# Seven products in three of four column groups of the down product, with sums carried in PSUM by ScalarE

## The chip, the cores and the metric

The kernel runs on one core of one Trainium2 chip. The metric is the device time of one execution in microseconds; the time before is the median of three runs, 1151.33 us (1150.51 to 1153.75). A profile was taken of one further execution.

## The reference

One layer on 256 tokens plus 16 meta tokens, model width 2048, everything in float32. Attention (differential and stick-breaking heads) comes first; the change leaves it alone apart from where its tables lie. What follows it is what matters here:

```python
m = _rmsnorm(h, g_mlp[l])
hid = jnp.square(jax.nn.relu(jnp.einsum('bld,df->blf', m, w_up[l])))   # 2048 -> 8192
h = h + jnp.einsum('blf,fd->bld', hid, w_down[l])                      # 8192 -> 2048
```

## The kernel before

**Precision.** Every float32 operand is split into a high part, rounded by ScalarE (a cast, L169), and a low part, what is left of it, by VectorE (a subtraction, L171). A product is then three matmuls: high by high, low by high and high by low. In the names, `raw` is a loaded block of weights (128 x 1024 values), `whi` and `wlo` its two parts, `m` the normalised input, `hid` the hidden values.

**Stages.** First the projections and attention, then the output product (L1038 with `out`), then the MLP. The MLP is cut into 8 rounds of 1024 hidden columns. In a round, four strips of `up` products (L1032) make the hidden values, each strip from four blocks of weights; `down` products (L1038) take the round's hidden values times the weights of four column groups u = 0 to 3 of the output, four blocks each. I call a block of up weights **c**, and a block of down weights in a plain group **d**: 24 matmuls 256 wide for c, 12 matmuls 512 wide for d.

**Seven products.** For the groups in `FAST`, a 2 x 2 block product is done with seven products in place of eight (`fast_a`, `fast_b`). A loaded block gives two sets of parts: **a** (the three blocks as they are, 9 matmuls 256 wide) and **b** (four sums of blocks, made by VectorE in L267 to L271 in place in `raw`, 12 matmuls 256 wide). The hidden values need four more sums for it (`up_evac`, L856 to L860), which all strips make. The seven results of a group stand in four PSUM banks. After a round, `fast_evac` moves them out: ScalarE copies them to the tile `z` in the first round (L896), VectorE adds them to `z` in all others (L899). After the last round `combine` turns the seven sums into four and adds them to the residual `H` (L918, L922). A plain group is added to `H` by VectorE every round (`plain_evac`, L876).

**Order.** All engines run in an order that is written when the program is built. TensorE follows the list `order`; in a round the next round's up blocks lie between the down blocks of this one. `Pace` counts expected times of the engines and puts the jobs of ScalarE and VectorE (casts, subtractions, evacuations) into their queues accordingly; each engine then works strictly through its queue. A block's parts go into one of `MLP_PARTS` sets of buffers, in turn: the first three sets come from the pool `weights`, the others from the pool `mlp`. The cast of block g waits until TensorE has done block g - MLP_PARTS. Loads are issued by SyncE, five `raw` buffers in turn.

**Tables.** The tile `cst` (identity, rotation tables, masks) lies in the pool `const`, which stays to the end; the pool `temps` is given up after attention.

Of the kernel before, what the change touches and what calls it, by code (L numbers as in the profile page):

```python
# [21 lines left out]
ROUNDS = 8  # L22
PAIRS = 4
# [2 lines left out]
KINDS = ((0, 3, 1, 2, 4, 5), (1, 0, 2, 4, 3, 5), (1, 0, 2, 4, 3, 5), (1, 0, 4, 3, 2, 5))  # L26
PARTS = 3
LEAD = 2
MLP_PARTS = 5
MLP_LEAD = 4  # L30
FAST = {(r, u) for r in range(ROUNDS) for u in (0, 2)}
PSUM_BANKS = {"acc": 4, "att": 4}
SLOTS = {"k": 4, "q": 4, "v": 2, "e": 3, "pr": 2, "ah": 2, "m": 2, "n": 2}
K0 = META + P
# [1 line left out]
SW = K0 + TOK  # L36
SEG = (slice(TOK, SW), slice(0, TOK))

C_ID, C_COS, C_SIN, C_MD, C_MS, C_BLK, C_SEL, C_END = 0, 128, 400, 672, 800, 1216, 1344, 1346
G_MIX, G_MLP, G_Q, G_K, G_D, G_S, G_L, G_END = 0, 16, 32, 33, 34, 35, 36, 292  # L40


# [77 lines left out]
def hymba_layer(ctx: ExitStack, tc: tile.TileContext, xT_d, xh_d, win_d, wout_d, wup_d, wdn_d, cst_d, par_d, out_d):  # L120
    nc = tc.nc
    cp = ctx.enter_context(tc.tile_pool(name="const", bufs=1))
# [15 lines left out]
    def bank(tag, name):  # L138
        return ps.tile([P, 512], F32, tag=tag, bufs=PSUM_BANKS[tag], name=name)
# [12 lines left out]


    par = cp.tile([P, G_END], F32, name="par")
    cst = cp.tile([P, C_END], F32, name="cst")
    xT = big.tile([P, KT, TOK], F32, tag="x", name="xT")
    um = big.tile([P, KT, 2, TOK], F32R, tag="act", name="u")
    mixed = big.tile([P, KT, 2, SEQ], F32R, tag="mix", name="mixed")
# [36 lines left out]
    for i in range(PAIRS):
        order += up(0, i, range(4))
    for r in range(ROUNDS):
        for u in (0, 2):
            ab, d = down(r, u, range(PAIRS)), down(r, u + 1, range(PAIRS))
            if r < ROUNDS - 1:  # L200
                c = up(r + 1, u, range(4)) + up(r + 1, u + 1, range(4))
                for p in range(PAIRS):
                    order += [c[2 * p], ab[2 * p], c[2 * p + 1], ab[2 * p + 1], d[p]]
            else:
                order += [*ab[:4], d[0], *ab[4:6], d[1], *ab[6:], *d[2:]]
    index = {key: g for g, key in enumerate(order)}
    loads = [g for g, key in enumerate(order) if key[0] != "b"]
    load_of = {g: n for n, g in enumerate(loads)}
# [90 lines left out]
    for c in range(4):  # L299
        n = 2 if c == 0 else 4  # L300
# [8 lines left out]

    def constants():  # L310
        yield from later(RAW)
        pc.at["cst"] = load(cst, cst_d, C_END)
        load(par[:, G_L:], par_d[:, G_L:], G_END - G_L)
        for g in range(RAW + 1, LEAD + RAW):
            pc.job("fetch", later(g))


    ident = cst[:, C_ID : C_ID + P]
    cos = cst[:, C_COS : C_COS + TOK]
    sin = cst[:, C_SIN : C_SIN + TOK]  # L320
    maskd = cst[:, C_MD : C_MD + P]
    masks = cst[:, C_MS : C_MS + SW]
    blk64 = tp.tile([P, P], F32R, bufs=1, name="blk64")
    sel = cst[:, C_SEL : C_SEL + 2]
    ones = cp.tile([P, P], F32R, name="ones")
    gqk = tp.tile([P, 2], F32, bufs=1, name="gqk")
    gout = cp.tile([P, 2], F32, name="gout")
    nlam = cp.tile([P, 1], F32, name="nlam")
# [553 lines left out]

    LAST_FAST = {u: max(r for r, v in FAST if v == u) for u in {u for _, u in FAST}}

    def fast_evac(r, u, o):

        new = u not in Z
        if new:
            Z[u] = mtile(f"z{u}", [P, 7 * 256], f"z_{u}")
        z = Z[u]  # L890
        yield pc.pe, "a" if new else "v"
        for i in range(4):
            n = 512 if i < 3 else 256
            dst = z[:, 512 * i : 512 * i + n]
            if new:
                nc.scalar.copy(dst, o[i][:, :n])  # L896
                t = pc.A(n)
            else:
                nc.vector.tensor_tensor(dst, o[i][:, :n], dst, op=ALU.add)  # L899
                t = pc.V(n)  # L900
            pc.give("att", t)
            yield pc.pe, "a" if new else "v"
# [25 lines left out]
    def banks(tag, n, name):  # L928
        while sum(t <= pc.pe for t in pc.banks[tag]) < n:
            pc.pe += 100  # L930
            pc.pump()
        pc.banks[tag] = sorted(pc.banks[tag])[n:]
        return [bank(tag, f"{name}_{j}") for j in range(n)]
# [36 lines left out]
        yield from gen  # L970
        pc.give("e", max(pc.pe, pc.dve, pc.act) + pc.WAIT)

    idle = cp.tile([P, 512], mybir.dt.bfloat16, name="idle")
    nc.vector.memset(idle, 0.0)
    warm = bank("att", "warm")
    for _ in range(WARM):
# [94 lines left out]
    for g in range(first_mlp, len(order)):  # L1071
        what, r, u, p = order[g]
        begin(g, MLP_LEAD)
        hi, lo = parts[g]
        pc.stall(("w", g, 3))
        if what == "up":
            if p == 0:
                open_strips["up", r, u] = banks("acc", 1, f"up_{r}_{u}")[0]
            o = open_strips["up", r, u]
            for j in range(2):  # L1080
                for kk in range(4):
                    k = 2 * p + kk % 2 + 8 * (kk // 2)
                    pc.stall(("m", k))
                    w = [x[:, kk, P * j : P * j + P] for x in (hi, lo)]
                    t = triple2(o[:, SEQ * j : SEQ * j + SEQ], w, m[:, k], p == 0 and kk == 0 and j == 0, p == 3 and kk == 3)
                    pc.pump()
            if p == 3:
                pc.job("evac", after(t, up_evac(r, u, o)))
        else:
            fast = (r, u) in FAST  # L1090
            pc.stall(("hid", r, p))
            x = lambda slot: [hid[r][:, p, slot, a] for a in range(2)]
            if p == 0 and what == "a":
                open_strips["down", r, u] = banks(*(("att", 4) if fast else ("acc", 2)), f"down_{r}_{u}")
# [81 lines left out]
```

## Time and profile before

| | |
|---|---|
| median of three runs | 1151.33 us |
| the profiled execution, its own time | 1152.82 us |
| its span, first to last instruction | 1150.9 us |
| TensorE busy | 1133.8 us, 8383 matmuls |
| VectorE busy | 928.1 us, 1420 instructions |
| ScalarE busy | 710.1 us, 1103 instructions |
| mean granted TensorE clock | 0.995 |

The MLP's matmuls run from 433.5 us to 1145.1 us of the span. A busy TensorE is not a TensorE at its peak, since the profile's matmuls overlap; the start-to-start distance of matmuls is the better measure. "Idle before" is the time in which an engine waited, and the name after the arrow is what it waited for.

### The profile page before, as it was taken

The page shows a single profiled execution, that of the slowest core. Times are in us where ns is not written, and L with a number is a line of the kernel's source. Part 1 is how long each engine was busy: PE and PEld are TensorE (multiplying, and loading weights), DVE is VectorE, ACT ScalarE, POOL GpSimd, SP SyncE. Part 2 cuts the span into 40 slices and gives each one's busy share as a digit, 9 for nine tenths or more (in the row PEclk, how much of TensorE's full clock was granted, in tenths as well). Part 3 has the DMA queues.
Part 4 walks back from the last instruction along what each step waited for, and adds up shares of the span by engine and source line. Part 5 has one row for each costly group of instructions (what it writes and reads, how often), then busy time and mean ns, then how long its engine had stood idle before and what let it go on. Part 6 is the DMA issues. An engine that isn't in the chain of part 4 may idle for free. (4 is left out here: it accounts for less than half of the span.)

```text
span 1150.9 us, 21193 instructions
## 1 busy us (share of the span) xinstructions
PE 1133.8 (99%) x8383; PEld 1076.6 (94%) x8383; DVE 928.1 (81%) x1420; ACT 710.1 (62%) x1103; POOL 1.1 (0%) x8
## 2 busy tenths in 40 slices
PE   9999999999999999999999999999999999999987
PEld 8999999999998889999999999999999999999876
DVE  6987987987976556677878888888888888888788
ACT  7769888778776445556655555555555555555542
POOL 0000000000000000000000000000000000000000
PEclk9999999999999999999999999999999999999989
DMA  8564544554545555556566666566666656666543
GB/s 326 184 220 142 153 139 151 156 155 153 164 139 175 183 185 191 172 185 201 189 196 201 188 191 200 192 188 204 192 189 200 195 188 199 196 191 196 171 136 122
DMA packets 57987, 209.97 MB, mean 182 GB/s; under 512 B 6560, under 2 KB 6688, under 8 KB 57760
## 3 DMA queue, kind: packets, MB, share of 16 engines
q1 hardware_dynamic: 57888, 208.61, 57.1%
q8 instruction: 66, 1.08, 0.4%
q14 instruction: 33, 0.27, 0.1%
HBM read 206.49 MB, written 2.10 MB: 181 GB/s over the span
## 5 line engine op out<-in xcount | busy, mean ns | idle before, releaser
L169 ACT CAST whi<-raw 128x1024 fp32r<-128x1024 f32 (+2 forms) x454 | 455.8, 1008 | 374.8 <-PE up L1032 198.7
L171 DVE TENSOR_TENSOR wlo<-raw,whi 128x1024 fp32r<-128x1024 f32 (+2 forms) x454 | 525.2, 1170 | 171.7 <-ACT whi L169 154.3
L1032 PE MATMUL up<-m,whi 128*128 128x256 f32 x2048 | 366.2, 281 | 1.3 <-DVE m L813 0.9
L1038 PE MATMUL down<-whi,hid 128*128 128x256 f32 (+1 forms) x1408 | 324.2, 324 | 7.1 <-DVE z L899 7.1
L1032 PEld LDWEIGHTS up<-m,whi 128*128 128x128 f32 x2048 | 319.3, 190 | 6.8 <-DVE m L813 1.6
L1032 PE MATMUL up<-m,wlo 128*128 128x256 f32 x1024 | 287.3, 281 | 0.0
L1038 PEld LDWEIGHTS down<-whi,hid 128*128 128x128 f32 x1408 | 232.3, 191 | 25.8 <-issue 3.6
L1038 PE MATMUL down<-wlo,hid 128*128 128x256 f32 (+1 forms) x704 | 228.1, 324 | 0.9 <-DVE wlo L171 0.9
L947 PE MATMUL acc<-u,whi 128*128 128x272 f32 (+1 forms) x768 | 224.6, 292 | 0.4 <-ACT whi L169 0.4
L949 PE MATMUL acc<-u,wlo 128*128 128x272 f32 (+1 forms) x768 | 221.0, 288 | 0.2 <-DVE wlo L171 0.2
L948 PE MATMUL acc<-u,whi 128*128 128x272 f32 (+1 forms) x768 | 220.6, 287 | 0.0
L1032 PEld LDWEIGHTS up<-m,wlo 128*128 128x128 f32 x1024 | 194.9, 190 | 0.0
L947 PEld LDWEIGHTS acc<-u,whi 128*128 128x128 f32 x768 | 145.9, 190 | 2.3 <-ACT whi L169 1.3
L949 PEld LDWEIGHTS acc<-u,wlo 128*128 128x128 f32 x768 | 145.6, 190 | 0.7 <-DVE wlo L171 0.7
L948 PEld LDWEIGHTS acc<-u,whi 128*128 128x128 f32 x768 | 146.2, 190 | 0.0
L1038 PEld LDWEIGHTS down<-wlo,hid 128*128 128x128 f32 x704 | 134.2, 191 | 11.9 <-DVE wlo L171 1.1
L1038 PE MATMUL out<-whi,mixed 128*128 128x512 f32 x256 | 79.8, 393 | 0.0
L1038 PEld LDWEIGHTS out<-whi,mixed 128*128 128x128 f32 x256 | 47.2, 188 | 9.3
L1038 PE MATMUL out<-wlo,mixed 128*128 128x512 f32 x128 | 50.0, 390 | 0.0
L267 DVE TENSOR_TENSOR raw<-raw 128x512 f32<-128x512 f32 x64 | 44.3, 692 | 2.2
L868 DVE TENSOR_TENSOR hid<-hx,hid 128x1024 fp32r<-128x1024 f32 x32 | 38.9, 1216 | 0.0
L899 DVE TENSOR_TENSOR z<-down,z 128x512 f32<-128x512 f32 (+1 forms) x56 | 34.0, 615 | 0.0
(241 smaller groups left out, 844.4 us busy)
## 6 DMA issues: line engine op xcount, KB each, us to landing
raw<-in_wup SPq DMA_DIRECT2D x128, 512.0 KB, 3.6
raw<-in_wdn SPq DMA_DIRECT2D x128, 512.0 KB, 4.4
raw<-in_win SPq DMA_DIRECT2D x95, 512.0 KB, 3.7
raw<-in_wout SPq DMA_DIRECT2D x32, 512.0 KB, 3.5
H<-in_xh SPq DMA_DIRECT2D x1, 2048.0 KB, 8.3
out<-H SPq DMA_DIRECT2D x8, 256.0 KB, 2.1
xT<-in_x SPq DMA_DIRECT2D x3, 544.0 KB, 9.6
cst<-in_cst SPq DMA_DIRECT2D x1, 673.0 KB, 11.2
```

The lines of the kernel that those rows point to most:

```text
L169: nc.scalar.copy(hi, src)
L171: nc.vector.tensor_tensor(lo, src, as32(hi), op=ALU.subtract)
L267: nc.vector.tensor_tensor(raw[:, 3::-3], first, raw[:, 3:1:-1], op=ALU.add)
L868: nc.vector.tensor_tensor(lo, x, as32(hi), op=ALU.subtract)
L899: nc.vector.tensor_tensor(dst, o[i][:, :n], dst, op=ALU.add)
L947: nc.tensor.matmul(o, lhsT=h, rhs=xh, start=first, stop=False)
L948: nc.tensor.matmul(o, lhsT=h, rhs=xl, start=False, stop=False)
L949: nc.tensor.matmul(o, lhsT=l, rhs=xh, start=False, stop=last)
L1032: nc.tensor.matmul(out, lhsT=w[a], rhs=x[:, b], start=first and i == 0, stop=last and i == 2, skip_group_check=True)
L1038: nc.tensor.matmul(out, lhsT=x[a], rhs=w[b], start=first and i == 0, stop=last and i == 2, skip_group_check=check)
```

## The change

`FAST` holds groups 0, 1 and 2 in rounds 0 to 6 and group 0 alone in round 7: 22 pairs of round and group, 16 before. The order of blocks is a string of letters per group; in round 0 two strips are woven into each other, and the last round begins with two plain blocks and ends with two. The parts of blocks go into four sets of buffers, five before, and are made three blocks ahead, four before. A third tile `z` takes the place. The sums of a group over the rounds no longer grow in `z` by VectorE's additions: ScalarE copies the finished banks to `z` of this group and copies the `z` of the next group into the same banks, and the matmuls go on adding there, with no start flag after round 0. The tables, `ones` and `idle` move to `temps`; only the identity stays.

```diff
-MLP_PARTS = 5
-MLP_LEAD = 4
-FAST = {(r, u) for r in range(ROUNDS) for u in (0, 2)}
+MLP_PARTS = 4
+MLP_LEAD = 3
+FAST = {(r, u) for r in range(ROUNDS - 1) for u in range(3)} | {(ROUNDS - 1, 0)}
...
-    cst = cp.tile([P, C_END], F32, name="cst")
+    cst = tp.tile([P, C_ID], F32, bufs=1, name="cst")
+    ident = cp.tile([P, P], F32, name="ident")
...
-                c = up(r + 1, u, range(4)) + up(r + 1, u + 1, range(4))
-                for p in range(PAIRS):
-                    order += [c[2 * p], ab[2 * p], c[2 * p + 1], ab[2 * p + 1], d[p]]
-            else:
-                order += [*ab[:4], d[0], *ab[4:6], d[1], *ab[6:], *d[2:]]
+    order += up(0, 0, range(3)) + up(0, 1, range(3)) + up(0, 0, (3,)) + up(0, 1, (3,)) + up(0, 2, range(4)) + up(0, 3, range(4))
+    for r in range(ROUNDS - 1):
...
+        for u, mix in ((0, "cdcabcabcabcab"), (1, "cdcabcabcabcab"), (2, "cdcabcabcdabccab")):
...
+    order += [next({"d": d, "a": ab, "b": ab}[x]) for x in "dd" + "adbd" * 4 + "dd"]
...
+        after = fast_units[fast_units.index((r, u)) + 1 :][:1]
+        for i in AT:
...
+            yield pc.pe, "a"
+            nc.scalar.copy(Z[u][:, at], o[i][:, :n])
...
+            for r2, u2 in after:
+                new[i] = bank("att", f"down_{r2}_{u2}_{i}")
+                if u2 in Z:
+                    nc.scalar.copy(new[i][:, :n], Z[u2][:, at])
...
-                               p == 0 and (at, half) in ((0, 0), (1, 0), (3, 0), (2, 1)), p == PAIRS - 1, True)
+                               r == 0 and p == 0 and (at, half) in ((0, 0), (1, 0), (3, 0), (2, 1)), p == PAIRS - 1, True)
```

Three places show what moves. The first is VectorE's queue in the middle of a round, where the sums of an up strip's hidden values (`hx`) come by. Blocks are numbered from 128, where the MLP begins. Before, in round 2, 235 is an a, 237 its b, 236 and 238 are c and d:

```order
L171 TENSOR_TENSOR wlo_235_8360<-raw_235_8251,whi_235_8359 128x768
L267 TENSOR_TENSOR raw_235_8251<-raw_235_8251 128x2x256
L269 TENSOR_TENSOR raw_235_8251<-raw_235_8251 128x256
L271 TENSOR_TENSOR raw_235_8251<-raw_235_8251 128x256
L171 TENSOR_TENSOR wlo_236_8394<-raw_236_8313,whi_236_8393 128x1024
L171 TENSOR_TENSOR wlo_237_8411<-raw_235_8251,whi_237_8410 128x1024
L856 TENSOR_TENSOR hx_3_0_8405<-hx_3_0_8405 128x2x128
L858 TENSOR_TENSOR hx_3_0_8405<-hx_3_0_8405 128x128
L860 TENSOR_TENSOR hx_3_0_8405<-hx_3_0_8405 128x128
L171 TENSOR_TENSOR wlo_238_8434<-raw_238_8320,whi_238_8433 128x1024
L868 TENSOR_TENSOR hid_3_8455<-hx_3_0_8405,hid_3_8455 128x8x128
```

Here the b's subtraction (`wlo_237`) is ahead of the hidden sums, and another subtraction lies between these and `hid`. VectorE's queue in the changed kernel, at the same place in round 3, where 299 is an a, 300 its b and 301 a c:

```order
L172 TENSOR_TENSOR wlo_299_9858<-raw_299_9711,whi_299_9857 128x768
L268 TENSOR_TENSOR raw_299_9711<-raw_299_9711 128x2x256
L270 TENSOR_TENSOR raw_299_9711<-raw_299_9711 128x256
L272 TENSOR_TENSOR raw_299_9711<-raw_299_9711 128x256
L857 TENSOR_TENSOR hx_4_1_9868<-hx_4_1_9868 128x2x128
L859 TENSOR_TENSOR hx_4_1_9868<-hx_4_1_9868 128x128
L861 TENSOR_TENSOR hx_4_1_9868<-hx_4_1_9868 128x128
L172 TENSOR_TENSOR wlo_301_9893<-raw_301_9778,whi_301_9892 128x1024
L172 TENSOR_TENSOR wlo_300_9874<-raw_299_9711,whi_300_9873 128x1024
L869 TENSOR_TENSOR hid_4_9659<-hx_4_1_9868,hid_4_9659 128x8x128
```

The three sums of hidden values stand ahead of both subtractions, of which the later, `wlo_300`, is what TensorE needs first, and its own subtraction `hid` comes right behind it.

The second place is the evacuation of group 0. Before, in round 2, VectorE does it, with other work in between:

```order
L899 TENSOR_TENSOR z_0_6735<-down_2_0_0_8233,z_0_6735 128x512
L171 TENSOR_TENSOR wlo_247_8645<-raw_245_8494,whi_247_8644 128x1024
L856 TENSOR_TENSOR hx_3_1_8639<-hx_3_1_8639 128x2x128
L858 TENSOR_TENSOR hx_3_1_8639<-hx_3_1_8639 128x128
L860 TENSOR_TENSOR hx_3_1_8639<-hx_3_1_8639 128x128
L899 TENSOR_TENSOR z_0_6735<-down_2_0_1_8234,z_0_6735 128x512
L171 TENSOR_TENSOR wlo_248_8666<-raw_248_8554,whi_248_8665 128x1024
L899 TENSOR_TENSOR z_0_6735<-down_2_0_2_8235,z_0_6735 128x512
L868 TENSOR_TENSOR hid_3_8455<-hx_3_1_8639,hid_3_8455 128x8x128
L171 TENSOR_TENSOR wlo_249_8702<-raw_249_8584,whi_249_8701 128x1024
L899 TENSOR_TENSOR z_0_6735<-down_2_0_3_8236,z_0_6735 128x256
```

The four additions are spread over VectorE's row. In the changed kernel, in round 3, it stands in ScalarE's queue between two casts (293 is an a, 294 its b):

```order
L170 CAST whi_293_9701<-raw_293_9586 128x768
L900 COPY z_0_6602<-down_3_0_0_9387 128x512
L905 COPY down_3_1_0_9714<-z_1_6926 128x512
L900 COPY z_0_6602<-down_3_0_1_9403 128x512
L905 COPY down_3_1_1_9730<-z_1_6926 128x512
L900 COPY z_0_6602<-down_3_0_3_9423 128x256
L905 COPY down_3_1_3_9747<-z_1_6926 128x256
L900 COPY z_0_6602<-down_3_0_2_9452 128x512
L905 COPY down_3_1_2_9753<-z_1_6926 128x512
L170 CAST whi_294_9741<-raw_293_9586 128x1024
```

Four additions of VectorE have become eight copies of ScalarE, four out of PSUM and four into it, in one row; VectorE has none of it left.

The third place is the end of VectorE's queue, behind the MLP's last weights (`z_2` is group 2, `down_7_3` the last plain group). Before:

```order
L876 SCALAR_TENSOR_TENSOR H_1128<-down_7_1_1_13052,R2_116,H_1128 128x512
L899 TENSOR_TENSOR z_2_7214<-down_7_2_0_13211,z_2_7214 128x512
L899 TENSOR_TENSOR z_2_7214<-down_7_2_1_13212,z_2_7214 128x512
L899 TENSOR_TENSOR z_2_7214<-down_7_2_2_13213,z_2_7214 128x512
L899 TENSOR_TENSOR z_2_7214<-down_7_2_3_13214,z_2_7214 128x256
L918 TENSOR_TENSOR z_2_7214<-z_2_7214 128x256 x7
L922 SCALAR_TENSOR_TENSOR H_1128<-z_2_7214,R2_116,H_1128 128x256 x4
L876 SCALAR_TENSOR_TENSOR H_1128<-down_7_3_0_13278,R2_116,H_1128 128x512
L876 SCALAR_TENSOR_TENSOR H_1128<-down_7_3_1_13279,R2_116,H_1128 128x512
```

The last fast group's evacuation and sums come ahead of the last plain additions. VectorE's queue in the changed kernel, at its end:

```order
L172 TENSOR_TENSOR wlo_469_13809<-raw_469_13745,whi_469_13808 128x1024
L172 TENSOR_TENSOR wlo_470_13825<-raw_470_13730,whi_470_13824 128x1024
L172 TENSOR_TENSOR wlo_471_13844<-raw_471_13764,whi_471_13843 128x1024
L924 TENSOR_TENSOR z_0_6602<-z_0_6602 128x256 x7
L928 SCALAR_TENSOR_TENSOR H_1130<-z_0_6602,R2_117,H_1130 128x256 x4
L877 SCALAR_TENSOR_TENSOR H_1130<-down_7_3_0_13826,R2_117,H_1130 128x512
L877 SCALAR_TENSOR_TENSOR H_1130<-down_7_3_1_13827,R2_117,H_1130 128x512
```

The last group's evacuation and sums, which stood behind the last subtraction of weights, are those of group 0 now, whose matmuls end three plain blocks before the last; behind them stand only the two additions of a plain group.

More of the change, by code (lines that the diff above doesn't have):

```diff
@@ L37 @@
 SEG = (slice(TOK, SW), slice(0, TOK))
-C_ID, C_COS, C_SIN, C_MD, C_MS, C_BLK, C_SEL, C_END = 0, 128, 400, 672, 800, 1216, 1344, 1346
+C_COS, C_SIN, C_MD, C_MS, C_BLK, C_SEL, C_ID, C_END = 0, 272, 544, 672, 1088, 1216, 1218, 1346
 G_MIX, G_MLP, G_Q, G_K, G_D, G_S, G_L, G_END = 0, 16, 32, 33, 34, 35, 36, 292
@@ L193, in down @@
         return [(x, r, u, p) for p in ps for x in ("ab" if (r, u) in FAST else "a")]
[L195 to L200, printed above, removed]
-                c = up(r + 1, u, range(4)) + up(r + 1, u + 1, range(4))
-                for p in range(PAIRS):
-                    order += [c[2 * p], ab[2 * p], c[2 * p + 1], ab[2 * p + 1], d[p]]
-            else:
-                order += [*ab[:4], d[0], *ab[4:6], d[1], *ab[6:], *d[2:]]
+    order += up(0, 0, range(3)) + up(0, 1, range(3)) + up(0, 0, (3,)) + up(0, 1, (3,)) + up(0, 2, range(4)) + up(0, 3, range(4))
+    for r in range(ROUNDS - 1):
+        c = iter([key for i in range(PAIRS) for key in up(r + 1, i, range(4))])
+        d = iter(down(r, 3, range(PAIRS)))
+        for u, mix in ((0, "cdcabcabcabcab"), (1, "cdcabcabcabcab"), (2, "cdcabcabcdabccab")):
+            ab = iter(down(r, u, range(PAIRS)))
+            order += [next({"c": c, "d": d, "a": ab, "b": ab}[x]) for x in mix]
+        assert not [*c, *d]
+    ab = iter(down(ROUNDS - 1, 0, range(PAIRS)))
+    d = iter([key for u in (1, 2, 3) for key in down(ROUNDS - 1, u, range(PAIRS))])
+    order += [next({"d": d, "a": ab, "b": ab}[x]) for x in "dd" + "adbd" * 4 + "dd"]
     index = {key: g for g, key in enumerate(order)}
@@ L311, in constants @@
         yield from later(RAW)
-        pc.at["cst"] = load(cst, cst_d, C_END)
+        pc.at["cst"] = load(cst, cst_d[:, :C_ID], C_ID)
+        load(ident, cst_d[:, C_ID : C_ID + P], P)
         load(par[:, G_L:], par_d[:, G_L:], G_END - G_L)
@@ L315, in constants @@
             pc.job("fetch", later(g))
-    ident = cst[:, C_ID : C_ID + P]
     cos = cst[:, C_COS : C_COS + TOK]
@@ L324, in hymba_layer @@
     sel = cst[:, C_SEL : C_SEL + 2]
-    ones = cp.tile([P, P], F32R, name="ones")
+    ones = tp.tile([P, P], F32R, bufs=1, name="ones")
     gqk = tp.tile([P, 2], F32, bufs=1, name="gqk")
@@ L883, in hymba_layer @@
     LAST_FAST = {u: max(r for r, v in FAST if v == u) for u in {u for _, u in FAST}}
+    fast_units = sorted(FAST)
+    AT = (0, 1, 3, 2)
     def fast_evac(r, u, o):
-        new = u not in Z
-        if new:
+        if u not in Z:
             Z[u] = mtile(f"z{u}", [P, 7 * 256], f"z_{u}")
[L890 to L902, printed above, removed]
+        after = fast_units[fast_units.index((r, u)) + 1 :][:1]
+        for r2, u2 in after:
+            open_strips["down", r2, u2] = new = {}
+        for i in AT:
+            at = slice(512 * i, min(512 * i + 512, 7 * 256))
+            n = at.stop - at.start
+            yield pc.pe, "a"
+            nc.scalar.copy(Z[u][:, at], o[i][:, :n])
+            t = pc.A(n)
+            for r2, u2 in after:
+                new[i] = bank("att", f"down_{r2}_{u2}_{i}")
+                if u2 in Z:
+                    nc.scalar.copy(new[i][:, :n], Z[u2][:, at])
+                    t = pc.A(n)
+        for key in after:
+            pc.at["seed", *key] = t
         if r == LAST_FAST[u]:
@@ L971, in delayed @@
         pc.give("e", max(pc.pe, pc.dve, pc.act) + pc.WAIT)
-    idle = cp.tile([P, 512], mybir.dt.bfloat16, name="idle")
+    idle = tp.tile([P, 512], mybir.dt.bfloat16, bufs=1, name="idle")
     nc.vector.memset(idle, 0.0)
@@ L1093, in hymba_layer @@
             if p == 0 and what == "a":
-                open_strips["down", r, u] = banks(*(("att", 4) if fast else ("acc", 2)), f"down_{r}_{u}")
+                if fast and (r, u) == fast_units[0]:
+                    open_strips["down", r, u] = dict(zip(AT, banks("att", 4, f"down_{r}_{u}")))
+                elif fast:
+                    pc.stall(("seed", r, u))
+                else:
+                    open_strips["down", r, u] = banks("acc", 2, f"down_{r}_{u}")
             o = open_strips["down", r, u]
```

## The prediction

> **What bounds the kernel now.** I first read the busy times of the page:
>
> ```profile
> PE 1133.8 (99%) x8383; PEld 1076.6 (94%) x8383; DVE 928.1 (81%) x1420; ACT 710.1 (62%) x1103; POOL 1.1 (0%) x8
> ```
>
> TensorE works nearly all the time. Second I cut the time from the MLP's first matmul on into four stretches: the first round's up products, rounds 0 to 6, round 7, and what is left behind the last matmul. The columns are length, then busy time of PE, PEld, DVE, ACT and POOL, the granted clock, the DMA share and GB/s.
>
> ```profile
> 433.50:483.90 50.40, 49.08 (x394) 48.07 (x393) 32.18 (x42) 27.62 (x35) 0.00 (x0) 0.97 0.53 176
> 483.90:1088.60 604.70, 604.70 (x4527) 576.23 (x4526) 498.47 (x628) 337.52 (x371) 0.00 (x0) 1.00 0.62 194
> 1088.60:1145.10 56.50, 48.39 (x278) 42.37 (x276) 52.94 (x83) 22.46 (x25) 0.00 (x0) 0.94 0.37 122
> 1145.10:1150.90 5.80, 0.00 (x0) 0.00 (x0) 2.69 (x6) 0.00 (x0) 0.00 (x0) 0.94 0.49 181
> ```
>
> In rounds 0 to 6 TensorE never waits (604.70 of 604.70): time changes there only if matmuls go away, if they follow each other faster or slower, or if a wait comes that isn't there now. VectorE is busy for 82%, ScalarE for 56%. In round 7 VectorE is busy for 52.94 of 56.50 and TensorE waits: there VectorE is the bound.
>
> Third the timeline of TensorE, for the length of one block of each kind (start to start):
>
> ```profile
> 700.83 0.40 PE L1032 MATMUL up<-m,whi 128*128 128x256 f32 x2
> 701.06 0.28 PE L1032 MATMUL up<-m,wlo 128*128 128x256 f32 x1
> ...
> 703.70 0.40 PE L1038 MATMUL down<-whi,hid 128*128 128x256 f32 x2
> ...
> 704.78 0.39 PE L1032 MATMUL up<-m,whi 128*128 128x256 f32 x2
> ...
> 707.50 0.40 PE L1038 MATMUL down<-whi,hid 128*128 128x256 f32 x2
> ...
> 708.92 0.63 PE L1038 MATMUL down<-whi,hid 128*128 128x512 f32 x2
> ...
> 711.68 0.40 PE L1032 MATMUL up<-m,whi 128*128 128x256 f32 x2
> ```
>
> c 2.87, a 1.08, the second c 2.72, b 1.42, d 2.76 (2.77 over the round). The two c are the same 24 matmuls. The first has its parts in a set of buffers of the pool `weights`, the second in one of the pool `mlp`.
>
> **The change, part by part.** The sum is made against the profiled execution, 1152.82 us; its span is 1150.9, and the median of the runs is 1.49 lower.
>
> *Start.* Round 0's fourth up block waits for the last rows of `m`:
>
> ```profile
> PEld up L1032 <- DVE m L813: 1.6, 3, 1.1
> PE up L1032 <- DVE m L813: 0.9, 1, 0.9
> PEld up L1032 <- ACT m L811: 0.7, 2, 0.5
> PE up L1032 <- ACT m L811: 0.3, 1, 0.3
> ```
>
> These are 3.5 us, and the granted clock of this stretch is .97, so .03 x 50.4 = 1.5 are lost to slow matmuls besides. The new order puts three blocks of the second strip ahead of that block, 3 x 2.87 = 8.6 us of work that needs none of these rows and covers the wait. Between -3.5 and -5.0 I take -4.0, since some of the low clock may have another cause.
>
> *Pace in rounds 0 to 6.* Seven more groups are fast. Each trades four d, 4 x 2.77 = 11.08, for four a and b, 4 x (1.08 + 1.42) = 10.00: 7 x 1.08 = -7.6. Against it, four sets in place of five, three of `weights` and one of `mlp`: by the order, 62 of the 128 c lie in sets of `mlp` before and 18 after. 44 c at 2.87 in place of 2.72 are +6.6. Together -1.0. All buffers lie elsewhere now, since `cst`, `ones` and `idle` left `const`, and no row shows these places; the bounds are the two paces seen: the 110 other c at 2.72 as well, 16.5 lower, or the last 18 at 2.87, 2.7 higher (a and b, .12 us a matmul, already have the slow one). I take the value by sets.
>
> *Round 7.* It is bound by the chain of weights through VectorE:
>
> ```profile
> ACT whi L169 <- PE down L1038: 18.1, 9, 4.8
> PE down L1038 <- DVE z L899: 7.1, 3, 3.4
> PEld down L1038 <- issue: 3.6, 1, 3.6
> ```
>
> TensorE waits for the additions to `z` (7.1), ScalarE's casts stand still behind TensorE (18.1), and matmuls after a gap run slow (0.94 in the third stretch). The blocks themselves are 8 x 2.77 + 8 x 2.50 = 42.2 and a last d of round 6, 44.9; 56.5 - 44.9 = 11.6 are lost. Behind the last matmul stands a tail:
>
> ```profile
> 1144.81 1.67 DVE L922 SCALAR_TENSOR_TENSOR H<-z,R,H 128x256 f32<-128x256 f32 x4
> 1146.39 1.40 DVE L876 SCALAR_TENSOR_TENSOR H<-down,R,H 128x512 f32<-128x512 f32 x2
> 1147.16 0.99 SPq L880 DMA_DIRECT2D out<-H  x2
> ```
>
> From the end of round 6 it is now 56.5 + 5.8 - 2.8 (the last d of round 6 lies in it) = 59.5. After: twelve d and four pairs, 12 x 2.77 + 4 x 2.50 = 43.2. VectorE's share of it: twelve subtractions of 1.13, four pairs of .98 + 1.53 + 1.13 (rows below), sums of the last group 2.67 + 1.67, six additions of .7, in all 36.7, less than 43.2, so it no longer binds; I leave .5 for waits. The tail is the last d's second addition alone, a hop of .1 (as that of the casts) and .74 (half of 1.40 and the pipeline's end), and 3.1 from the end of VectorE (1147.79) to that of the span: 3.9. Sum 47.6, -11.9. If all 11.6 stayed lost, only the tail would be shorter, 1.9, and the blocks longer, 1.0: -.9 is the other end; I stay with the first, since VectorE's load falls below TensorE's.
>
> *VectorE in rounds 0 to 6.* It loses the additions to `z`, all 56 of this row (42 of them here, the rest in round 7):
>
> ```profile
> L899 DVE TENSOR_TENSOR z<-down,z 128x512 f32<-128x512 f32 (+1 forms) x56 | 34.0, 615 | 0.0
> ```
>
> and for each new fast group gains four times the sums and a subtraction, less two additions of .7 and a smaller subtraction. The durations, start to start (the first row is the cast behind the c that ends at 703.70, two casts in 1.92):
>
> ```profile
> 703.78 1.92 ACT L169 CAST whi<-raw 128x1024 fp32r<-128x1024 f32 x2 [0.88 <-PE up L1032]
> ...
> 1112.45 0.84 ACT L169 CAST whi<-raw 128x768 fp32r<-128x768 f32 x1 [1.30 <-PE down L1038]
> 1113.32 0.96 DVE L171 TENSOR_TENSOR wlo<-raw,whi 128x768 fp32r<-128x768 f32 x1 [0.72 <-ACT whi L169]
> ...
> 1127.14 0.95 DVE L171 TENSOR_TENSOR wlo<-raw,whi 128x768 fp32r<-128x768 f32 x1
> 1128.12 0.69 DVE L267 TENSOR_TENSOR raw<-raw 128x512 f32<-128x512 f32 x1
> 1128.85 0.42 DVE L269 TENSOR_TENSOR raw<-raw 128x256 f32<-128x256 f32 x1
> 1129.31 0.43 DVE L271 TENSOR_TENSOR raw<-raw 128x256 f32<-128x256 f32 x1
> 1129.65 0.48 DVE L922 SCALAR_TENSOR_TENSOR H<-z,R,H 128x256 f32<-128x256 f32 x1
> 1130.05 1.22 DVE L171 TENSOR_TENSOR wlo<-raw,whi 128x1024 fp32r<-128x1024 f32 x1
> 1131.18 0.48 DVE L922 SCALAR_TENSOR_TENSOR H<-z,R,H 128x256 f32<-128x256 f32 x1
> ```
>
> Subtraction of an a .98, the three sums 1.53, a subtraction of 1024 values 1.13. So 4 x (1.53 + 1.13 - .15) - 1.4 = 8.6 a group, 60 for seven; less 42 x .61 = 26: 498 + 34 = 532 of about 604, 88%. It doesn't bind as a sum. It binds where a chain is longer than the work of TensorE that covers it. With four sets the cast of an a starts when the block four before it is done. Where a pair comes behind a c and VectorE takes up the hidden sums between (the first place shown above), the chain up to the b's subtraction is: cast .08 (703.70 to 703.78) + .84, hop .03, subtraction .98, sums 1.53, hidden sums, two subtractions. The hidden sums are these rows, .45 + .33 + .21 = .99:
>
> ```profile
> 700.69 0.42 DVE L856 TENSOR_TENSOR hx<-hx 128x256 f32<-128x256 f32 x1
> 701.14 0.29 DVE L858 TENSOR_TENSOR hx<-hx 128x128 f32<-128x128 f32 x1
> 701.47 0.29 DVE L860 TENSOR_TENSOR hx<-hx 128x128 f32<-128x128 f32 x1
> 701.68 0.68 DVE L899 TENSOR_TENSOR z<-down,z 128x512 f32<-128x512 f32 x1
> ```
>
> Together 3.46 + .99 + 1.13 + 1.22 = 6.80. TensorE meanwhile does a, b, c and a, 1.08 + 1.42 + 2.87 + 1.08 = 6.45, and the b's first two matmuls need only the high part, .24 more (700.83 to 701.06): 6.69. The wait is .11, or .26 with c at 2.72, and as much again for the hops between engines that I don't see; .22 taken. It comes once for each of the four strips; once the subtraction `hid` (behind `wlo_300` there) delays the next pair too, and walking the two queues row by row with these durations leaves .57. That is 3 x .22 + .57 = 1.2 a round, x 7 = +8.6. Pairs without hidden sums have 5.81 against 6.69 and .88 to spare. The bounds are 0, if VectorE does some of it earlier, and, with .4 more in every chain, 7 x 4 x .4 = 11 above mine. The same walk along the queues before, with five sets, gives no wait, which the second stretch bears out.
>
> *ScalarE.* 42 evacuations by VectorE become copies, and seeds go back. Copies out have rows:
>
> ```profile
> 528.21 0.58 ACT L896 COPY z<-down 128x512 f32<-128x512 f32 x1
> 528.68 1.05 ACT L866 CAST hid<-hx 128x1024 fp32r<-128x1024 f32 x1
> ```
>
> .47 start to start. Copies into PSUM have no row. They lie between .47 (the nearest: the same engine, size and memory, the other way) and 1.05 (a cast of twice the size); I take .47. Six copies of 512 and two of 256 are 6 x .47 + 2 x .28 = 3.4, behind a cast of .84. Queued behind them is the next b's cast, which starts late. TensorE has c, d and c to do before the next group's a, 2.87 + 2.77 + 2.87 = 8.5, so 4 us are left over: no cost. At .8 each the four copies into PSUM take 1.3 more, and by the walk the first b of a round comes 1.15 late, since two c and the first pair follow each other closely there. The Trainium skill, "ScalarE: Activation LUTs", section "Step-by-step: what each stage is for", says that ScalarE writes PSUM faster than SBUF; by this the copy would cost .47 or less and the sum stay as it is, and no run here shows it.
>
> *Loads* are as many as before, 32 a round, and SyncE's queue holds little else.
>
> ```profile
> raw<-in_wdn SPq DMA_DIRECT2D x128, 512.0 KB, 4.4
> ```
>
> Five `raw` in turn, 86.4 us a round (604.7 / 7): 13.5 us for one, 4.4 of it to land, and a pair holds it for its chain of 6.8. 2.3 are left: hidden.
>
> The sum: 1152.82 - 4.0 - 1.0 - 11.9 + 8.6 = 1144.5; on the median's basis 1143.0.
>
> **Rivals.**
>
> *No new waits* (B). VectorE, free of additions, runs ahead and the .22 don't arise: 1143.0 - 8.6 = 1134.4. For it: the wait is a fifth of a subtraction. Against: the chain has no slack in it.
>
> *The pace doesn't hang on the buffers* (P). Then the 6.6 aren't lost, and with shorter c the waits grow by 1.6: 1138. Against it stand the 2.87 and 2.72 above. The Trainium skill, "TensorE: Matmul & The Clock Gate", Part 2, "Step-by-step", step 1, says that the streaming operand and the weight load have a read port each and don't disturb each other, so by it the buffers' place would not matter. By that rule 1138; the trace disagrees with it by .15 in a c.
>
> *Round 7 stays half bound by VectorE* (F): half of the 11.6 of waits stays, +5.8: 1148.8. For it: twelve plain blocks bring no relief to casts that come late. Against: VectorE's 36.7 of 43.2.
>
> *Seeds late* (C). At .8 a copy 7 x 1.15 = +8: 1151; at 1.0, by the same walk, 7 x 1.96 = +14: 1157. For it: no row has such a copy. Against: the copy the other way at .47.
>
> *Four sets are too few* (D), the other side. If each chain is x longer than I count, the 28 pairs with hidden sums wait x longer and the 56 others x - .88. With one more cast ahead in ScalarE's queue (x = .96, half of the 1.92) that is 27 + 4: 1174. It decides from x = .42 on, 1154.8. For it: a set less, so that a cast hangs on the block just done, and VectorE at 88%. Against: the five sets leave no gap at 82%.
> The Trainium skill, "Perfetto Trace Analysis", "Optimization Strategy", says that the same gap repeating on the engine that should be full can mean too few buffers; before there is no gap to show it.
>
> **Chances.** Forecast .42, B .12, P .10, F .10, C .12, D .14. A measurement here can tell .3% from no change, 1147.9 and 1154.8 being the bounds. Faster: forecast, B and P, .64. Same: F and C, .22 (C at .8). Slower: D, .14. The forecast's own range is 1138 to 1148 (round 7 and the waits by 5 each). The range goes down to 1133 for B with a little of the faster pace, up to 1153 for C, and leaves out D and less than a tenth below.
>
> **What would show it.** The first stretch has no waits of `up` on `m`, and a clock near 1. In rounds 0 to 6 short gaps of .2 to .6 ahead of a b, four a round, released by `wlo`; many more and all alike is D, none is B. c at 2.87 and 2.72 by set, else P or other places. The last round at 47.6 with the clock at 1.00, else F. No wait of an a or b after the copies, else C. It would be wrong above all if the four sets' chain has a hop that I don't see, or if the new places of the buffers have a pace of their own.

## The result and the profile after

The changed kernel takes 1145.91 us (median of 5 runs, 1145.76 to 1147.94), the kernel before in the same comparison 1151.59. The ratio is 0.995, with a 95% interval of 0.9936 to 0.9965. The forecast was 1143.0, in a range from 1133 to 1153. The profiled execution takes 1145.84 us, its span 1144.0; the sum made against 1152.82 had given 1144.5.

The busy times of the changed kernel's page, and then its stretches: the first round's up products, rounds 0 to 6, round 7, and what is behind the last matmul (columns as in the prediction):

```profile
PE 1131.5 (99%) x8599; PEld 1082.5 (95%) x8599; DVE 950.1 (83%) x1459; ACT 799.2 (70%) x1283; POOL 1.1 (0%) x8
```

```profile
433.50:479.80 46.30, 46.30 (x393) 46.28 (x392) 30.03 (x38) 26.64 (x34) 0.00 (x0) 1.00 0.60 194
479.80:1096.40 616.60, 610.99 (x4791) 591.36 (x4790) 538.12 (x697) 426.81 (x546) 0.00 (x0) 1.00 0.58 190
1096.40:1140.20 43.80, 43.49 (x230) 36.48 (x228) 39.53 (x62) 23.50 (x31) 0.00 (x0) 1.00 0.51 172
1140.20:1144.00 3.80, 0.00 (x0) 0.00 (x0) 0.74 (x1) 0.00 (x0) 0.00 (x0) 1.00 0.37 138
```

The first stretch is 46.3 us, 4.1 less. Round 7 with its tail is 43.8 + 3.8 = 47.6, 11.9 less than the 59.5 of before; the granted clock there is 1.00. The middle is to be set against the kernel before up to the end of the last block of round 6:

```profile
483.90:1091.30 607.40, 607.40 (x4538) 578.27 (x4536) 501.10 (x631) 338.88 (x373) 0.00 (x0) 1.00 0.62 193
```

It grew by 9.2 us, although there are 1.08 us less of matmuls in each of seven rounds. TensorE now waits in it (610.99 busy of 616.60). For whom, over the whole MLP:

```profile
PEld down L1044 <- DVE wlo L172: 12.0, 29, 0.7
PE down L1044 <- DVE wlo L172: 4.5, 14, 0.4
PEld down L1044 <- ACT down L905: 0.2, 1, 0.2
```

PEld and PE count the same gap twice in part, so the sum is read elsewhere: of 88 b blocks, 28 take 1.6 to 2.1 us from start to start, where the others take 1.36 to 1.45. They are four a round, in the same four places each (the last pair of group 0, the last two of group 1, the second of group 2, in round 6 the last of group 2 instead). Their excess is 12.8 us over 1.42. Summed from the steps between their matmuls it is 13.0: 10.0 of waiting, and 2.9 because the first matmul behind each wait takes .22 to the next one in place of .12.

One of them, in round 3, with the rows of ScalarE, VectorE and TensorE (the first DVE row is three subtractions, the last of which is that of the a):

```profile
785.12 0.84 ACT L170 CAST whi<-raw 128x768 fp32r<-128x768 f32 x1 [0.51 <-PE up L1038]
783.36 3.59 DVE L172 TENSOR_TENSOR wlo<-raw,whi 128x1024 fp32r<-128x1024 f32 x3
786.98 0.69 DVE L268 TENSOR_TENSOR raw<-raw 128x512 f32<-128x512 f32 x1
...
788.51 0.42 DVE L857 TENSOR_TENSOR hx<-hx 128x256 f32<-128x256 f32 x1
...
789.50 2.35 DVE L172 TENSOR_TENSOR wlo<-raw,whi 128x1024 fp32r<-128x1024 f32 x2
791.77 1.22 DVE L869 TENSOR_TENSOR hid<-hx,hid 128x1024 fp32r<-128x1024 f32 x1
...
784.99 0.28 PE L1044 MATMUL down<-whi,hid 128*128 128x256 f32 x1
...
791.19 0.28 PE L1044 MATMUL down<-wlo,hid 128*128 128x256 f32 x1
791.31 0.40 PE L1044 MATMUL down<-whi,hid 128*128 128x256 f32 x2
791.90 0.39 PE L1044 MATMUL down<-wlo,hid 128*128 128x256 f32 x1 [0.20 <-DVE wlo L172]
792.13 0.40 PE L1044 MATMUL down<-whi,hid 128*128 128x256 f32 x2
```

The c ends at 784.99, where the next block begins, and frees its set. The cast starts at 785.12, the sums run from 786.98 to 788.51, the hidden sums to 789.50, two subtractions to 791.85. That is 6.86 us; the forecast had 6.80. TensorE has reached the b at 791.31 after 6.32 us and would have taken up `wlo` .24 later. It starts at 791.90, and the next matmul follows .23 later, where the two ahead of the b (791.19, 791.31) are .12 apart. Nothing is idle in VectorE's row between 786.98 and 792.99: it is a chain, and one with no slack.

### The profile page after: what moved, and what is told of

It reads as the page before. It is cut to its first block, busy times and chain, and to the rows that moved or that the text cites. A ratio compares the mean times of both kernels' runs of the same rounds, so it can differ in the third digit from the quotient of the medians.

```text
span 1144.0 us, 21838 instructions
## 1 busy us (share of the span) xinstructions
PE 1131.5 (99%) x8599; PEld 1082.5 (95%) x8599; DVE 950.1 (83%) x1459; ACT 799.2 (70%) x1283; POOL 1.1 (0%) x8
## 4 chain that ended last, share of the span: by engine, by line
PE 81%; DVE 15%; issue 2%; ACT 2%; DMA 1%; SPq 0%; DVEq 0%; ACTq 0%
PE up L1038 25%; PE down L1044 19%; PE acc L953 8%; DVE wlo L172 8%; PE acc L955 8%; PE acc L954 8%; PE out L1044 8%; DVE raw L268 2%; ACT whi L170 2%; DVE raw L270 1%; DVE raw L272 1%; DVE hid L869 1%; DVE hx L857 1%; PE s_d L603 1%; PE po_s L643 1%
## 5 line engine op out<-in xcount | busy, mean ns | idle before, releaser
L170 ACT CAST whi<-raw 128x1024 fp32r<-128x1024 f32 (+2 forms) x478 | 470.6, 997 | 277.1 <-PE up L1038 82.4
L172 DVE TENSOR_TENSOR wlo<-raw,whi 128x1024 fp32r<-128x1024 f32 (+2 forms) x478 | 543.9, 1158 | 137.3 <-ACT whi L170 133.0
L1038 PE MATMUL up<-m,whi 128*128 128x256 f32 x2048 | 369.9, 282 | 0.0
L1044 PEld LDWEIGHTS down<-whi,hid 128*128 128x128 f32 x1552 | 247.7, 189 | 11.8 <-ACT down L905 0.2
L1044 PE MATMUL down<-wlo,hid 128*128 128x256 f32 (+1 forms) x776 | 238.2, 307 | 5.9 <-DVE wlo L172 4.5
L1044 PEld LDWEIGHTS down<-wlo,hid 128*128 128x128 f32 x776 | 146.6, 189 | 18.5 <-DVE wlo L172 12.0
L268 DVE TENSOR_TENSOR raw<-raw 128x512 f32<-128x512 f32 x88 | 60.9, 692 | 3.0
L900 ACT COPY z<-down 128x512 f32<-128x512 f32 (+1 forms) x88 | 45.5, 528 | 0.1
L905 ACT COPY down<-z 128x512 f32<-128x512 f32 (+1 forms) x76 | 40.9, 538 | 2.4
```

Of the source, the lines that this page charges most:

```text
L170: nc.scalar.copy(hi, src)
L172: nc.vector.tensor_tensor(lo, src, as32(hi), op=ALU.subtract)
L268: nc.vector.tensor_tensor(raw[:, 3::-3], first, raw[:, 3:1:-1], op=ALU.add)
L900: nc.scalar.copy(Z[u][:, at], o[i][:, :n])
L905: nc.scalar.copy(new[i][:, :n], Z[u2][:, at])
L1038: nc.tensor.matmul(out, lhsT=w[a], rhs=x[:, b], start=first and i == 0, stop=last and i == 2, skip_group_check=True)
```

## The experiments

All ratios are to the kernel before, with their 95% intervals.

**The start alone.**

```diff
-    for i in range(PAIRS):
-        order += up(0, i, range(4))
+    order += up(0, 0, range(3)) + up(0, 1, range(3)) + up(0, 0, (3,)) + up(0, 1, (3,)) + up(0, 2, range(4)) + up(0, 3, range(4))
```

> The kernel before with the changed order of round 0 alone. Theory of the forecast: the waits of up products for the last rows of m go, and nothing else: 4.0 us less, a ratio of 0.9965; the stretch from the first up block to the first of round 1 falls from 50.4 to 46.4 us, the rest keeps its length. Rival: the second strip's blocks come before their weights are split, so the waits go to the weights: 1 us less at most, 0.999.

Measured: 1148.76 us, ratio 0.9974 (0.9965 to 0.9983).

```profile
433.50:479.90 46.40, 46.40 (x394) 46.28 (x393) 32.72 (x43) 27.39 (x35) 0.00 (x0) 1.00 0.57 188
479.90:1085.00 605.10, 605.10 (x4530) 576.55 (x4529) 498.60 (x628) 337.53 (x371) 0.00 (x0) 1.00 0.62 194
```

The first stretch is what it is in the changed kernel, TensorE is busy in all of it by the profile, and the clock is 1.00 where it was 0.97. By the starts of the matmuls two early c still take .4 to .5 longer than others of their sets, here and in the changed kernel. The spans differ by 4.0 (1150.9 and 1146.9), the medians by 2.9; 4.0 lies at the edge of the interval.

**The last round alone.** `FAST` keeps groups 0 and 2 in rounds 0 to 6, five sets, VectorE's additions; only round 7 changes.

```diff
-FAST = {(r, u) for r in range(ROUNDS) for u in (0, 2)}
+FAST = {(r, u) for r in range(ROUNDS - 1) for u in (0, 2)} | {(ROUNDS - 1, 0)}
...
+    order += [next({"d": d, "a": ab, "b": ab}[x]) for x in "dd" + "adbd" * 4 + "dd"]
```

> The kernel before with the changed last round alone (group 0 fast, three plain groups, the new string of blocks); rounds 0 to 6 as before, five sets, VectorE adding to z. Theory of the forecast: from the end of round 6 to the end of the span 47.6 us in place of 59.5, 11.9 less, a ratio of 0.9897. Rival: in the changed kernel the end is short because VectorE has no additions to z left in its queue; here they are still there, and group 2's sums come in as well, so half of the waits stay: 6 us less, 0.995.

Measured: 1140.49 us, ratio 0.9905 (0.989 to 0.992), 11.2 us less. The stretch from the end of round 6 to the end of the span, and TensorE's waits from 1088 on:

```profile
1090.70:1138.30 47.60, 43.35 (x229) 36.77 (x227) 42.68 (x68) 16.70 (x17) 0.00 (x0) 1.00 0.44 144
```

```profile
PEld down L1039 <- DVE z L900: 0.6, 1, 0.6
PE down L1039 <- DVE z L900: 0.4, 1, 0.4
```

The stretch is 47.6 us, as forecast. TensorE waits once, for 0.6, on an addition to `z`; before it was 7.1 there, and 11.6 in all with the clock. So the gain of the end needs no PSUM sums: fewer fast groups in the last round and an order that ends plainly make it.

**The weights 64 bytes later, in the kernel before.**

```diff
+    wp.tile([P, 16], F32, tag="pad", bufs=1, name="pad_w")
+    sp.tile([P, 16], F32, tag="pad", bufs=1, name="pad_s")
```

> The kernel before with 64 bytes of padding ahead of the weight buffers and 64 behind them: the three sets of the pool weights begin 64 bytes later, so that no set begins at the same place modulo 128 bytes as m; order, pools and instructions stay. Theory of addresses: the 66 up blocks of these sets take 2.72 in place of 2.87 us, 9.9 less, a ratio of 0.9914, and the small a and b swap their two paces between even and odd rounds, which cancels. Rival theory of the pool or of the turn in the ring (what is slow is the set, not the address): no change, 1.000.

Measured: 1147.86 us, ratio 0.9968 (0.9955 to 0.998): 3.8 us less, not nothing and not 9.9. (A place is the address within a partition that the built program gives a tile, modulo 128 bytes; the traces don't hold it.) The starts of four blocks in round 2, c, a, c and b:

```profile
675.46 0.40 PE L1034 MATMUL up<-m,whi 128*128 128x256 f32 x2
678.21 0.39 PE L1040 MATMUL down<-whi,hid 128*128 128x256 f32 x2
679.23 0.40 PE L1034 MATMUL up<-m,whi 128*128 128x256 f32 x2
682.06 0.40 PE L1040 MATMUL down<-whi,hid 128*128 128x256 f32 x2
```

The c of the shifted set `weights` takes 2.75 here, 2.83 in other rounds, 2.87 before. The c of the set in `mlp`, which moved by 128 bytes, takes 2.83 in this round and 2.74 in the next, and 2.72 before. In round 0, where c follows c, all sets have 2.72 but for the waits (in the changed kernel with the same padding, shown below, most c of round 0 have 2.83). So the place decides part of it: at m's place it is 2.87, elsewhere 2.72 to 2.83. Which of these it is goes with the round's parity and the block ahead, and I have no rule for it.

**Five sets in the changed kernel.**

```diff
-MLP_PARTS = 4
-MLP_LEAD = 3
+MLP_PARTS = 5
+MLP_LEAD = 4
```

> The changed kernel with five sets of part buffers and parts made four blocks ahead, as before the change. Theory of the forecast: the chain of a pair behind an up strip gets one more block of cover, so the 28 waits ahead of a b go (12.8 us), and 30 more up blocks lie in sets at the fast place (30 x 0.15 = 4.5 us): 17 less than the changed kernel, 1129, a ratio to the kernel before of 0.980. Rival: the waits come from VectorE's load of 88%, which a fifth set doesn't lower; only the 4.5 go: 1141, 0.991.

Measured: 1131.25 us, ratio 0.9823 (0.981 to 0.9836), 14.7 us less than the changed kernel. The middle and all of TensorE's waits in the MLP:

```profile
479.90:1081.40 601.50, 601.50 (x4790) 587.34 (x4789) 533.92 (x695) 425.09 (x546) 0.00 (x0) 1.00 0.60 195
```

```profile
PE down L1044 <- ACT down L905: 0.7, 1, 0.7
PEld down L1044 <- ACT down L905: 0.9, 1, 0.9
```

The waits for `wlo` are gone, with VectorE as busy as before (533.92 of 601.5, 89%). Its load is not what made them. The only wait left is the last group's seed in round 7. The middle falls by 15.1. By the starts of the matmuls, 13.0 of it are the waits and 2.8 the c: 42 of the middle's 112 lie in sets of `mlp` now, 14 before, but 13 of the 42 run at 2.83 and not at 2.72. The a, b and d together take .7 more.

**The hidden sums later in VectorE's queue**, with four sets.

```diff
-            yield t, "v"
+            yield t + 5000, "v"
             nc.vector.tensor_tensor(x[:, 4:7:2], x[:, 0:2], x[:, 1:4:2], op=ALU.subtract)
```

> The changed kernel with the hidden sums of an up strip put 5 us later in VectorE's queue: in three of the four strips of a round they stand behind the b's subtraction that TensorE waited for, in one they come into the next pair's chain. Theory of the forecast (the chain of four sets with the hidden sums in it is what TensorE waits for): of four waits a round three go and one of 0.4 stays, so of 12.8 us in 28 waits about 3 in 7 stay: 1136.3, a ratio to the kernel before of 0.987. Rival: VectorE's load makes the waits and they only change place: 1144, 0.993.

Measured: 1134.81 us, ratio 0.985 (0.9836 to 0.9865).

```profile
PEld down L1044 <- DVE wlo L172: 2.3, 8, 0.4
PE down L1044 <- DVE wlo L172: 0.2, 1, 0.2
```

```profile
479.80:1086.20 606.40, 605.74 (x4790) 589.91 (x4789) 541.53 (x698) 429.81 (x546) 0.00 (x0) 1.00 0.60 193
```

With the same sets, places and work, 28 long b become 9, which by their starts cost 3.0 us in place of 13.0, and the middle falls by 10.2. So it was the place of the three sums, with the cast and the subtraction `hid` that follow them, and not the load, that made the waits. The one a round that was to stay is there (the last pair of group 1, .25 to .30). Beside it stand the last one of round 6, which was there before, and a new one of .40 in round 0.

**The sums over rounds by VectorE again**, all else as changed.

```diff
-            yield pc.pe, "a"
-            nc.scalar.copy(Z[u][:, at], o[i][:, :n])
-            t = pc.A(n)
+            yield pc.pe, "a" if fresh else "v"
+            ...
+                nc.vector.tensor_tensor(Z[u][:, at], o[i][:, :n], Z[u][:, at], op=ALU.add)
...
-                if u2 in Z:
-                    nc.scalar.copy(new[i][:, :n], Z[u2][:, at])
...
-                               r == 0 and p == 0 and (at, half)
+                               p == 0 and (at, half)
```

> The changed kernel with the sums over rounds kept in z by VectorE's additions again (ScalarE copies out in round 0 only, nothing goes back into PSUM, each round's matmuls start afresh); order, sets and groups as changed. Theory of the forecast: the 18 evacuations of rounds 1 to 6 stand in VectorE's queue ahead of a pair's chain, 3 x 0.60 + 0.34 = 2.1 us against 0.9 to spare, 1.3 us of wait each, 23 us more than the changed kernel: 1169, a ratio of 1.015. Rival: VectorE has room for them (38 us more on 534 of 612), and they are late nowhere: 1146, 0.995.

Measured: 1174.61 us, ratio 1.0186 (1.0166 to 1.0206), 29 us more than the changed kernel. One of its four runs took 1169.93, at a mean granted clock of 0.995, where the others had 0.991.

```profile
PE down L1046 <- DVE z L905: 16.7, 12, 2.1
PEld down L1046 <- DVE z L905: 13.4, 6, 2.3
PEld down L1046 <- DVE wlo L172: 12.3, 28, 0.7
PE down L1046 <- DVE wlo L172: 5.8, 20, 0.5
```

The waits for `z` stand at six places only, the first pair of group 0 in rounds 2 to 7, behind the evacuations of group 2. In round 2 (TensorE in the a and the b, VectorE's additions of group 2 and then of group 0, and the clock behind the waits):

```profile
665.88 0.47 PE L1046 MATMUL down<-whi,hid 128*128 128x256 f32 x2 [0.66 <-DVE z L905]
669.24 0.50 PE L1046 MATMUL down<-whi,hid 128*128 128x256 f32 x2 [2.06 <-DVE z L905]
...
662.19 0.68 DVE L905 TENSOR_TENSOR z<-down,z 128x512 f32<-128x512 f32 x1
665.06 1.01 DVE L905 TENSOR_TENSOR z<-down,z 128x512 f32<-128x512 f32 x2
668.50 0.68 DVE L905 TENSOR_TENSOR z<-down,z 128x512 f32<-128x512 f32 x1
...
692.77 2.21 DVE L905 TENSOR_TENSOR z<-down,z 128x512 f32<-128x512 f32 x4
...
670.30:673.50 3.20, 3.20 (x17) 3.20 (x16) 1.92 (x2) 1.05 (x1) 0.00 (x0) 0.50 0.41 133
```

The four additions of group 2 are spread over 7 us, with subtractions and sums of pairs between them, and the a and the b of group 0 each wait for a bank that VectorE has not read yet (in round 7 the a waits twice). PE's row counts both, 12 waits of 16.7 us; PEld's row has the longer one of each again. The additions of group 0 stand together, and nobody waits for `z` behind the other 12 evacuations. Behind five of the six places the granted clock falls to 0.50 for 3.4 us, once 6.8: 84 matmuls there are .21 apart in place of .12, 8.0 us more. Against the changed kernel the six places take 28.2 us longer, a, b and the next c together. The waits for `wlo` stay. So the expectation came near by luck: not 18 waits of 1.3 in a pair's chain, but six stops of 4.7 at the banks, over a quarter of it slow clock. The copies by ScalarE are worth 29 us in this order of VectorE's queue: without them three fast groups with their c d c between are slower than the kernel before. Whether group 2's additions, put together, would wait less, no run here shows.

**The weights 64 bytes later, in the changed kernel**, the two padding lines shown above.

> The changed kernel with the weight buffers 64 bytes later, as in the experiment with the kernel before: none of the four sets begins at m's place modulo 128 bytes. Theory that the place alone sets the pace: 110 up blocks at 2.72 instead of 2.87, 16.5 less, of which the 28 in a chain that waits gain nothing: 12 less than the changed kernel, 1134, a ratio of 0.985. Theory that a place other than m's gives 2.72 to 2.83, by what ran before, as the experiment on the kernel before showed: 0.08 a block, 110 - 28 blocks, and the 18 others 0.06 slower: 5.5 less, 1140.5, 0.990. Rival: no change, 0.995.

Measured: 1138.81 us, ratio 0.9883 (0.9867 to 0.99), 7.1 us less than the changed kernel, nearer to the 5.5 of the mixed paces than to 12.

```profile
PEld down L1046 <- DVE wlo L174: 14.3, 31, 0.7
PE down L1046 <- DVE wlo L174: 7.9, 29, 0.5
```

```profile
480.20:1089.90 609.70, 601.99 (x4791) 582.21 (x4790) 537.77 (x697) 426.81 (x546) 0.00 (x0) 1.00 0.59 192
```

The middle falls by 6.9, from 616.6. By the starts, its c take 9.3 less and the waits grow from 13.0 to 15.4 (the rows of PE and PEld, which count in part the same, from 12.0 + 4.5 to 14.3 + 7.9): a TensorE that runs faster covers less of a chain that stays 6.8 long, and part of the pace comes back as waits.

**Five sets and the weights 64 bytes later.** Both edits above.

> The changed kernel with five sets and the weight buffers 64 bytes later. No chain waits with five sets, so the pace comes out whole: 80 up blocks at 2.72 would be 12 less than with five sets alone (1131.25), 1119, a ratio of 0.972; with 2.72 to 2.83 by what ran before, 0.08 a block, 6 less, 1125, 0.977. Rival: no change, 0.982.

Measured: 1122.78 us, ratio 0.9747 (0.9733 to 0.9762), 8.5 less than with five sets alone.

```profile
479.50:1073.10 593.60, 593.60 (x4791) 579.91 (x4790) 533.26 (x694) 424.79 (x546) 0.00 (x0) 1.00 0.60 197
```

With no chain that waits, the middle keeps 7.9 us. All c but two that take longer at the start have 2.72 to 2.83 now, 115.3 ns a matmul in the mean of the middle.

**The hidden values of odd rounds later too.**

```diff
+        if r == 1:
+            mtile("pad", [P, 16], "pad_h")
         if r % 2:
             hid[r] = mtile("hid", [P, PAIRS, FULL, 2, P], f"hid_{r}", 1, F32R)
```

> The changed kernel with five sets and the weight buffers 64 bytes later, and with the hidden values of the odd rounds 64 bytes later too, so that hidden values and weights never begin at the same place modulo 128 bytes. Theory of places: a and b of the odd rounds, now at 118 to 120 ns a matmul, come to the 113 to 118 that they have in even rounds, 3.7 ns x 21 matmuls x 12 pairs x 3 rounds and a third of a round, 3 us less than without it (1122.8): 1119.5, a ratio to the kernel before of 0.972; if all came to 113, 6 less, 0.969. Rival: it holds for up products only, no change, 0.975.

Measured: 1122.52 us, ratio 0.9743 (0.973 to 0.9756): no change against 0.9747.

```profile
479.30:1072.60 593.30, 593.30 (x4790) 579.01 (x4789) 532.84 (x694) 425.18 (x546) 0.00 (x0) 1.00 0.59 197
```

The expectation missed, and not because nothing happened: read from the starts of the matmuls, b of odd rounds went from 119.9 to 116.4 ns, but d of odd rounds from 228.3 to 232.7, and c of odd rounds, whose own operands did not move, from 2.75 to 2.77 us. Over rounds 0 to 6 the a and b take 1.9 us less, the c and d 1.6 more.

**Start and end together, in the kernel before**: the edits of the first two experiments.

> The kernel before with the changed order of round 0 and the changed last round together; rounds 0 to 6 as before (two fast groups, five sets, sums by VectorE). Theory that the two gains are separate stretches and add up: 2.9 + 11.2 to 4.0 + 11.9 us less, 1136 to 1138, a ratio of 0.987; then rounds 0 to 6 of the changed kernel cost it 8 to 10 us against those of before, and the third fast group alone, in four sets, is a loss. Rival: start and end overlap or the middle gains in the changed kernel: 1146 or more, 0.995.

Measured: 1136.94 us, ratio 0.9869 (0.9856 to 0.9883), 15.3 less than before. The gains add up, and this kernel, with two fast groups, five sets and VectorE's sums, is 9 us faster than the changed one. Against it, the changed kernel with five sets (1131.25) is 5.7 faster: that is what a third fast group, with the copies by ScalarE that make room for it, is worth where next to nothing waits.

## Why the prediction held, and where its sizes were off

| step of the sum | forecast | profiled executions | what shows it |
|---|---|---|---|
| start | -4.0 | -4.1 | first stretch; the start alone, -2.9 (2.0 to 4.0) |
| rounds 0 to 6, fewer matmuls and their pace | -1.0 | -3.8 | 9.2 less the waits |
| rounds 0 to 6, new waits | +8.6 | +13.0 | steps in the 28 b; hidden sums later, 10.2 of it |
| round 7 and tail | -11.9 | -11.9 | last stretches; the end alone, -11.2 |
| sum | -8.3 | -6.9 | spans 1150.9 and 1144.0 |

*Start and end* came out as worked out, each in its own stretch, each alone as well. That VectorE's 36.7 of 43.2 us would no longer bind in round 7 was right: it is busy for 39.53 of 43.8, 2.8 more than counted, and TensorE's blocks set the time. The rival F is out. The low clock at the start, of which the forecast left a part to another cause, lies in one piece in the kernel before:

```profile
447.00:450.40 3.40, 3.40 (x18) 3.40 (x18) 0.00 (x0) 0.73 (x1) 0.00 (x0) 0.50 0.28 112
```

Half of these 3.4 us, 1.7, is lost there, and in the changed kernel it is not.

*The waits* stand where the walk along the queues had put them: four a round, ahead of a b behind an up strip, released by the b's subtraction, one of them the longest because `hid` stands in the next pair's chain. In even rounds they are .2 to .3 and .5 long, 1.22 us a round in the mean, for 1.23 forecast. The term was too low all the same, 8.6 for 13.0, in two steps. One the sum put at nothing: behind each wait a matmul takes .22 to the next in place of .12, 28 times, 2.9 us. The other is the cover: I took 1.08 + 1.42 + 2.87 + 1.08 = 6.45 for every round. In odd rounds a takes 1.02 and b 1.36, so it is 6.32 in the rows shown and 6.12 where the c is one of 2.72; the waits there are .3 to .6, 1.71 a round, 1.4 us more in three rounds. The rival B (no waits) is out, and so is D: at three of the four places the chain is 6.81 to 6.86, at most .06 longer than counted, not .4. (At the fourth it has `hid` in it, as the walk had.)

*The pace* was off the other way, -3.8 for -1.0, in part by the same oversight. The c cost 6.7 more, as counted (6.6). The additional a and b, at 1.02 and 1.36 in the sets of `weights` in odd rounds, took 2.1 less than at 1.08 and 1.42; and d, 2.78 each before and 2.76 now, gave 1.0 more than at 2.77. So the errors of these two terms, +4.4 and -2.8, cancelled in part, and that the sum came out nearer than they did was luck. Where a chain waits, a faster TensorE gains little; the shift of the weights in four and in five sets shows it (6.9 and 7.9 less in the middle, with 2.4 more of waits in the first). The rival P is out: a c still took 2.87 in the sets of `weights` and 2.72 in that of `mlp`, and moving the buffers changed it. The Trainium skill, "TensorE: Matmul & The Clock Gate", Part 2, step 1, gives the two operands read ports of their own, so that loading the one doesn't slow the other. Read as the prediction read it, that the place can't matter, four experiments disagree: matmuls 256 wide take 118 to 120 ns where both operands begin at one place modulo 128 bytes, 113 to 118 otherwise.

*Seeds* were hidden, as costed, though a copy costs more than I took:

```profile
800.01 0.58 ACT L900 COPY z<-down 128x512 f32<-128x512 f32 x1
800.62 0.59 ACT L905 COPY down<-z 128x512 f32<-128x512 f32 x1
801.14 0.58 ACT L900 COPY z<-down 128x512 f32<-128x512 f32 x1
```

A pair out and in takes 1.13 from start to start, where I had .94; eight copies take 4.1 in place of 3.4 (without the cast that stands between them here), with 4 us to spare. The only wait for a copy is .2 at the last group. The rival C is out. The Trainium skill, "ScalarE: Activation LUTs", "Step-by-step: what each stage is for", would have the way into PSUM as the faster; here it is .59 against .58, so no gain shows, though the two copies differ in their source as well.

*The small miss* of 1143.0 against 1145.91 has two parts: 1.4 in the sum, and 1.5 because I carried the difference of the profiled execution to the median over to the forecast, while the changed kernel's profiled execution lay at its median (1145.84).

That five sets clear the waits agrees with the Trainium skill, "Perfetto Trace Analysis", "Optimization Strategy", on the same gap that repeats. But another place for the hidden sums does most of it too (10.2 us), with four sets. The one gives the chain more cover, the other shortens it; neither was needed for the load.

The change as a whole gained 16.0 us at its ends and lost 9.2 in its middle. Four sets in place of five account for more than that loss: with a fifth set the same change gains 20 us (1131.25).

## What to carry to other kernels

Cost a chain through the shared buffers against the work that covers it, block by block in the order that the queue has, and not the load of the engine: at 89% VectorE cost nothing with five sets, and at 87% 13.0 us with four. Where a repeating wait of a few tenths stands ahead of a block, look for small work in its chain that nobody needs soon, and move it behind. Count a stop with what follows it: .1 us behind each short wait here, and behind the stops of 2 us with VectorE's sums some microseconds at half the granted clock. Try the parts of a large change alone: here the plain end and the woven start gave 15.3 us without the rest.

## What I had not expected

The pace of a matmul 256 wide was known from the trace before to depend on its buffers, 113 or 120 ns. New is that it takes other values too, that moving one set changes the pace of another (2.72 to 2.74 and 2.83 in `mlp`, when `weights` moved by 64 and `mlp` by 128 bytes), and that a gain for b can be a loss for c and d (116.4 for 119.9 and, for d, 232.7 for 228.3 ns). What sets the value between 113 and 118 is open; no run here was made to tell it. The fastest kernel of these runs has five sets and the shifted weights, 1122.5 to 1122.8 us, 2.5% below the kernel before.
